# Layer ends with VectorE and ScalarE in a fixed order, and later step sums and norms in the SSD layer

## Chip, cores and metric

One core of a Trainium2 chip runs the whole program. The metric is the device time of one execution in microseconds; the median of three runs before the change is 2514.39 (2512.95 to 2517.65).

## What is computed

Two blocks of two layers each on 512 positions of 1024 channels, in float32. Block 1 has two equal layers:

```
h = rms_norm(x, pre_norm[layer]);  proj = h @ w_in[layer]      # conv half b,c,x,z and retention half q,k,v,z
y_conv = c_b * conv3(c_c * c_x) * silu(c_z)
y_ret  = rms(retention(rotary(q), rotary(k), v)) * silu(r_z)
out = concat(y_conv, y_ret) @ w_out[layer]
x = x + rms_norm(out, post_norm[layer])
```

Block 2 puts 16 meta tokens in front (528 positions) and computes an SSD mixer, an MLP, an attention and a second MLP. Its SSD mixer is the part that matters here:

```
z, xbc, dt = split(h @ w_in);  xbc = silu(conv4(xbc));  dt = softplus(dt + bias)
a_cs = cumsum(dt * a) per chunk of 128                          # the step sums
y = chunk-wise state recurrence over xs, B, C with decay exp(a_cs differences)   # 8 groups of 4 heads
g = (y + xs * d) * silu(z);  g = g * rsqrt(mean(g*g) over the group) * norm_g     # the norm of a group
return g @ w_out
```

## The kernel before

All weights stream from memory in tiles of 1 MB (`Stream`, two buffers each of the raw tile `wraw`, its leading part `whi`, cast by ScalarE at L74, and the rest `wlo`, a difference by VectorE at L75). A product is three matmuls: leading part by leading part and the two mixed terms. Activations are split in the same way (`xh`/`xl` in `prep`, L261 and L262; `mh`/`ml` in `split`, L418 and L419). A framework's scheduler puts the instructions of each engine in order; the order of program text counts only as far as it decides between ready instructions. PSUM has eight banks: `pb0` to `pb3` and the like for dense products, four `side` banks (`C0`, `C1`, `D0`, `D1`) for everything else.

**The end of a layer of block 1.** The last two tiles of the output product (`ob` 2 and 3) run in halves of 256 positions (`duo`): both tiles for the first half, then both for the second. VectorE adds each result to `oS` (L812). ScalarE squares it; the squares of output tiles 0 to 5 are summed by POOL (`sums`, L428), and three `ones` matmuls (L817, L820) sum over the channels. Then `residual` (from L774) does for one half: square root on ScalarE and reciprocal on VectorE (L438) give the factor `rp`; four pairs of channels are scaled (L782), added to the residual (L784) and split for the next layer (L261 on ScalarE, L262 on VectorE); squares of the new residual are added (`sqx`, L793), summed by two `ones` matmuls (L795) and become the next layer's factor `R` (`Rx` after layer 1). The next layer begins with its c and x tiles, again in halves (L390 is the matmul of all products in halves), drained by VectorE at L628 with the factor; the SSD layer begins likewise with `sx` and `sbc` (drains at L941).

**The SSD layer.** `steps` computes dt (VectorE's chain ends at L896), sums it by two matmuls (L899 with a triangle, L900 with ones) and sends the transposed sums through memory (`acsD`), from where each chunk's `ab` is broadcast. A group projects xs, B, C and z (L382, drains L853 and L958), then loops over five chunks: `cb` (L983), ScalarE's decay and VectorE's `M` (L989), `xd` (L992), matmuls of y (L1003), `xw` and state. Then the sum of squares goes through memory: `gd`, `rs`, twelve small VectorE steps (L405 to L409), `ge`, and the broadcast `rb` (POOL issues them at L1044 to L1049). At the end of the group, in program order, VectorE multiplies `gz` by the gain and `rb` (L1063) and splits it for the output product:

```
for n in range(2):
    V.scalar_tensor_tensor(gz[n], gz[n], gcol(V_SNG, 2 * g + n), rb, ALU.mult, ALU.mult)
    m = mix_tile(f"s{g}{n}")
    split(m, gz[n], slice(0, T2))
    mix.append(m)
```

Of the kernel before, what the change touches and what calls it, by code (L numbers as in the profile page):

```python
# [31 lines left out]
class Stream:  # L32
# [75 lines left out]
    def next(self, key):  # L108
        i = self.pos
        assert self.plan[i][0] == key, (self.plan[i][0], key)  # L110
        while len(self.done) <= min(i + 1, len(self.plan) - 1):
# [4 lines left out]
        return r


def build(ctx, tc, a):
# [331 lines left out]
    with ExitStack() as c1:  # L451
# [167 lines left out]

        for l in range(2):  # L620

            mixc = []
            for p in range(4):
                cR = [tmp(f"cR{l}{p}{n}") for n in range(2)]
                if p == 0:
                    for _, os_, u, pss in duo([(l, "c", 0), (l, "x", 0)], X, META, load_x if l == 0 else None):
# [44 lines left out]
                if p == 3:  # L671
# [102 lines left out]
            def residual(i, o0, o1):  # L774

                rp = tmp(f"rp{l}{o0}")[:, : o1 - o0]
                rsqrt_mean(rp, (C0, C1)[i][:, :256], D)
                xs = slice(META + o0, META + o1)
                sp_ = (D0, D1)[i][:, :256]
                for k in range(0, 8, 2):  # L780
                    o2 = oS[:, k : k + 2, o0:o1]
                    V.tensor_tensor(o2, o2, rp.unsqueeze(1).to_broadcast([P, 2, o1 - o0]), ALU.mult)  # L782
                    for j in (k, k + 1):
                        V.scalar_tensor_tensor(xres[:, j, xs], oS[:, j, o0:o1], gcol(V_POST, 8 * l + j),  # L784
                                               xres[:, j, xs], ALU.mult, ALU.add)
                        prep(Xn, j, xs, gcol(gbase, j))

                sq = tmp(f"sqx{l}0{o0}")
                for k in range(0, 8, 2):
                    t = tmp(f"sqx{l}{k}{o0}") if k else sq  # L790
                    nc.scalar.activation(t.rearrange("p (n c) -> p n c", n=2), xres[:, k : k + 2, xs], AF.Square)
                    if k:
                        V.tensor_tensor(sq, sq, t, ALU.add)  # L793
                for n in range(2):
                    nc.tensor.matmul(sp_, ones, sq[:, 256 * n : 256 * n + 256], start=(n == 0), stop=(n == 1))  # L795
                rsqrt_mean(R[:, o0:o1] if l == 0 else Rx[:, xs], sp_, D)
                if l == 0:
                    V.tensor_tensor(RR[:, o0:o1], R[:, o0:o1], R[:, o0:o1], ALU.mult)

# [8 lines left out]
            for i, os_, u, pss in duo([(l, "ob", 2), (l, "ob", 3)], mixop(mixr), 0):  # L808
                sp_ = (C0, C1)[i][:, :256]
                for n in range(2):  # L810
                    k = 4 + 2 * u + n
# [1 line left out]
                    if u == 0:
                        sq_acc(sqt, sums[:, os_], k, oS[:, k, os_], f"sqp{l}{k}{i}")
                        continue
                    if k == 6:
                        nc.tensor.matmul(sp_, ones, sums[:, os_], start=True, stop=False)  # L817
# [748 lines left out]
```

## Time and profile before

| | |
|---|---|
| median of three runs | 2514.39 us |
| the profiled execution, time | 2515.09 us |
| the profiled execution, span | 2513.2 us |
| TensorE busy | 2448.3 us (97%) |
| VectorE busy | 1619.0 us (64%) |
| ScalarE busy | 1077.6 us (43%) |
| POOL busy | 151.6 us (6%) |
| mean granted TensorE clock | 0.991 |

The span runs from the first to the last instruction of the profiled execution. Busy shares are means over the whole span; a wait in one place is seen in windows and in the timeline, not in them. The granted clock tells which share of its full rate of 2.4 GHz TensorE was given: 1.00, or 0.50 for 1.2 GHz.

### The profile page before, as it was taken

The page shows a single profiled execution, that of the slowest core. Times are in us where ns is not written, and L with a number is a line of the kernel's source. Part 1 is how long each engine was busy: PE and PEld are TensorE (multiplying, and loading weights), DVE is VectorE, ACT ScalarE, POOL GpSimd, SP SyncE. Part 2 cuts the span into 40 slices and gives each one's busy share as a digit, 9 for nine tenths or more (in the row PEclk, how much of TensorE's full clock was granted, in tenths as well). Part 3 has the DMA queues.
Part 4 walks back from the last instruction along what each step waited for, and adds up shares of the span by engine and source line. Part 5 has one row for each costly group of instructions (what it writes and reads, how often), then busy time and mean ns, then how long its engine had stood idle before and what let it go on. Part 6 is the DMA issues. An engine that isn't in the chain of part 4 may idle for free.

```text
span 2513.2 us, 40393 instructions
## 1 busy us (share of the span) xinstructions
PE 2448.3 (97%) x16671; PEld 2189.0 (87%) x16671; DVE 1619.0 (64%) x2968; ACT 1077.6 (43%) x2046; POOL 151.6 (6%) x177
## 2 busy tenths in 40 slices
PE   8999999989999999889999999999999999999999
PEld 7888888878888888778999998999998566999999
DVE  6743555474435554877857889677675666966764
ACT  4422333333223334455625546245354675644432
POOL 1000000100000001022302200000011000000000
PEclk9999999999999999998999999999999999999999
DMA  4333222223332222233333332233221221332322
GB/s 147 106 100 97 82 82 76 79 78 91 100 103 74 84 84 68 69 92 90 90 106 95 88 88 90 88 96 98 94 92 49 63 69 38 96 104 95 109 84 85
DMA packets 220488, 220.90 MB, mean 88 GB/s; under 512 B 8972, under 2 KB 212877, under 8 KB 220304
## 3 DMA queue, kind: packets, MB, share of 16 engines
q1 hardware_dynamic: 215648, 207.50, 26.9%
q0 software_dynamic: 4176, 10.69, 1.8%
q8 instruction: 131, 2.15, 0.3%
q14 instruction: 53, 0.43, 0.1%
q10 hardware_dynamic: 480, 0.13, 0.0%
HBM read 215.47 MB, written 2.83 MB: 87 GB/s over the span
## 4 chain that ended last, share of the span: by engine, by line
PE 83%; DVE 9%; ACT 3%; DMA 2%; issue 2%; POOL 1%; ACTq 0%; SPq 0%; DVEq 0%; POOLq 0%
PE pb L382 44%; PE main L397 7%; PE side L334 6%; PE pb L397 4%; PE main L382 3%; PE main L334 3%; PE pb L334 3%; PE pb L390 2%; PE side L1404 1%; PE side L1420 1%; DVE wlo L75 1%; PE side L1012 1%; PE side L1003 1%; ACT whi L74 1%; PE main L1409 1%
## 5 line engine op out<-in xcount | busy, mean ns | idle before, releaser
L74 ACT CAST whi<-wraw 128x1024 fp32r<-128x1024 f32 (+2 forms) x301 | 302.7, 1045 | 614.6 <-PE pb L382 421.8
L75 DVE TENSOR_TENSOR wlo<-wraw,whi 128x1024 fp32r<-128x1024 f32 (+2 forms) x301 | 364.2, 1232 | 121.5 <-ACT whi L74 119.2
L382 PE MATMUL pb<-xl_n,whi 128*128 128x264 f32 (+1 forms) x1136 | 317.9, 330 | 0.0
L382 PE MATMUL pb<-xh_n,whi 128*128 128x264 f32 (+1 forms) x1136 | 317.4, 329 | 0.3 <-DVE zu L958 0.2
L382 PE MATMUL pb<-xh_n,wlo 128*128 128x264 f32 (+1 forms) x1136 | 315.3, 329 | 0.0
L382 PEld LDWEIGHTS pb<-xh_n,whi 128*128 128x128 f32 x1136 | 192.5, 189 | 20.3 <-issue 1.6
L382 PEld LDWEIGHTS pb<-xl_n,whi 128*128 128x128 f32 x1136 | 191.6, 189 | 19.7 <-issue 1.7
L382 PEld LDWEIGHTS pb<-xh_n,wlo 128*128 128x128 f32 x1136 | 191.8, 190 | 17.6 <-issue 0.2
L382 PE MATMUL pb<-xl_l,whi 128*128 128x512 f32 x416 | 164.9, 396 | 0.0
L382 PE MATMUL pb<-xh_l,wlo 128*128 128x512 f32 x416 | 164.9, 396 | 0.0
L382 PE MATMUL pb<-xh_l,whi 128*128 128x512 f32 x416 | 164.5, 395 | 0.0
L397 PE MATMUL main<-whi,mh_w 128*128 128x256 f32 x512 | 143.8, 281 | 0.3
L397 PE MATMUL main<-whi,ml_w 128*128 128x256 f32 x512 | 143.3, 281 | 0.0
L397 PE MATMUL main<-wlo,mh_w 128*128 128x256 f32 x512 | 143.2, 281 | 0.0
L103 ACT CAST whi<-wraw 128x1024 fp32r<-128x1024 f32 x64 | 65.8, 1047 | 139.5 <-issue 54.5
L90 ACT CAST wsh<-wsr 128x512 fp32r<-128x512 f32 x96 | 58.8, 618 | 106.9 <-DVE wsr L96 64.0
L382 PE MATMUL pb<-ml_u,whi 128*128 128x264 f32 x512 | 104.2, 285 | 0.2
L382 PE MATMUL pb<-mh_u,whi 128*128 128x264 f32 x512 | 103.8, 284 | 0.0
L382 PE MATMUL pb<-mh_u,wlo 128*128 128x264 f32 x512 | 103.6, 284 | 0.0
L397 PEld LDWEIGHTS main<-whi,mh_w 128*128 128x128 f32 x512 | 96.6, 189 | 1.1 <-ACT mh_w L418 0.9
L397 PEld LDWEIGHTS main<-whi,ml_w 128*128 128x128 f32 x512 | 96.7, 189 | 0.0
L397 PEld LDWEIGHTS main<-wlo,mh_w 128*128 128x128 f32 x512 | 96.1, 188 | 0.0
(687 smaller groups left out, 6522.4 us busy)
## 6 DMA issues: line engine op xcount, KB each, us to landing
wraw<-w_in SPq DMA_DIRECT2D x63, 1024.0 KB, 5.8
wraw<-mlp_w_up SPq DMA_DIRECT2D x32, 1024.0 KB, 5.5
wraw<-mlp_w_down SPq DMA_DIRECT2D x32, 1024.0 KB, 4.8
wraw<-w_out SPq DMA_DIRECT2D x16, 1024.0 KB, 4.8
wraw<-ssd_w_in SPq DMA_DIRECT2D x16, 1024.0 KB
wraw<-ssd_w_in SPq DMA_DIRECT2D x16, 512.0 KB, 5.3
ab<-acsD POOLq DMA_DIRECT2D x32, 256.0 KB, 3.8
kR<-ke SPq DMA_DIRECT2D x32, 132.0 KB, 3.0
```

The costliest lines, as they stand in the source:

```text
L74: nc.scalar.copy(hv[s], rv[s])
L75: eng.tensor_tensor(lv[s], rv[s], hv[s].bitcast(F32), ALU.subtract)
L90: nc.scalar.copy(h, sr[:, n])
L103: nc.scalar.copy(hi[:, c], raw[:, c])
L334: nc.tensor.matmul(ps, w[wq][a][:, k], X(xq, b, k), start=(k == 0 and wq + xq == 0), stop=(k == 3 and wq == 1))
L382: nc.tensor.matmul(ps, w[wq][:, k, wsl], x(xq, k, cs), start=(k == 0 and wq + xq == 0), stop=(k == nk - 1 and wq == 1))
L390: nc.tensor.matmul(ps, w[wq][:, k, wsl], x(xq, k, cs), start=(k == 0 and wq + xq == 0), stop=(k == nk - 1 and wq == 1))
L397: nc.tensor.matmul(ps, x(xq, k, ts_), w[wq][:, k, csl], start=(k == 0 and wq + xq == 0), stop=(k == nk - 1 and xq == 1))
L1003: nc.tensor.matmul(o, xd[:W, h], M[:W, h, :W], start=True, stop=(c == 0))
L1012: nc.tensor.matmul(st[:, :256], Bt[:W], xw[:W].rearrange("p h e -> p (h e)"), start=True, stop=True)
L1404: nc.tensor.matmul(sp_, Qh[:, h, q0 : q0 + M], Kh[:, h, :L], start=True, stop=False)
L1409: nc.tensor.transpose(pst[:, c, :M], p[:M, P * c : P * c + P], ident[:M, :M])
```

## The change

Four things are rewritten.

1. `residual` becomes the class `End` with its steps (`chain`, `pair`, `squares`, `factor`) as separate methods. They are called between the matmuls of the last products and of the next layer's first ones (`mm3k` takes a callback `mid`). Squares of the last four output tiles are no longer added by POOL; `chain` sums five pieces by `ones` matmuls.
2. `Ordered` ties all VectorE instructions, and all ScalarE instructions, from the first half's chain to the drains of the next layer's first tiles (in layer 1: of the SSD layer's) to the order of the program text. `inorder` does the same for single instructions.
3. The first tiles of the next layer (`entry`) use four pairs of banks, `pb0`/`pb1`, `pb2`/`pb3`, and the `side` banks `C0`/`C1`, instead of whatever comes free.
4. The step sums become a generator that stops before the two sums and before the rest, so that the sums' matmuls come after both z products of group 0; and `finish`, the norm of a group, is called in the next group's chunk 1 (for group 3 before the first output pass).

```diff
+    def end(self):
...
+        for engine in (mybir.EngineType.DVE, mybir.EngineType.Activation):
+            mine = [i for i in traced[n + 1 :] if i.engine == engine]
+            for p, q in zip(mine, mine[1:]):
+                self.tc.add_manual_dep(q, p.name, mybir.DependencyInfo(mybir.DependencyClass.NoSync,
+                                                                       mybir.DependencyReason.DATA), reason="order")
...
+            def chain(self, sqs):
+                ps = (C0, C1)[self.i][:, :256]
+                for n, sq in enumerate(sqs):
+                    inorder(nc.tensor.matmul(ps, ones, sq, start=(n == 0), stop=(n == len(sqs) - 1)))
+                self.rp = tmp(f"rp{self.l}{self.i}")[:, :256]
+                rsqrt_mean(self.rp, ps, D)
+
+            def pair(self, k):
+                o2 = oS[:, k : k + 2, self.os]
+                V.tensor_tensor(o2, o2, self.rp.unsqueeze(1).to_broadcast([P, 2, 256]), ALU.mult)
+                for j in (k, k + 1):
+                    V.scalar_tensor_tensor(xres[:, j, self.xs], oS[:, j, self.os], gcol(V_POST, 8 * self.l + j),
+                                           xres[:, j, self.xs], ALU.mult, ALU.add)
+                for j in (k, k + 1):
+                    prep(self.X, j, self.xs, gcol(self.g, j))
...
+        def entry(keys, x, ends):
...
+            banks = [[BANK[b + n][:, : cols[0].stop - cols[0].start] for n in range(2)] for b in (0, 2, 4, 0)]
...
+            mm(0, 0, (6, lambda: ends[1].chain(ends[1].sqs)))
+            for k in range(0, 8, 2):
+                ends[1].pair(k)
+                if k == 0:
+                    ends[0].squares()
+            if l:
+                yield
+            mm(1, 0)
+            ends[0].factor()
+            for u in range(2):
+                yield 0, slice(*PARTS[0]), u, banks[u]
+            ends[1].squares()
+            mm(0, 1)
+            ws.emit(len(ws.done))
+            ends[1].factor()
+            mm(1, 1)
+            for u in range(2):
+                yield 1, slice(*PARTS[1]), u, banks[2 + u]
+            order.end()
...
+            def first_end():
+                ends[0].chain(sqs)
+                order.begin()
+                ends[0].pair(0)
+
+            sqs1 = [sums[:, ends[1].os]] + last(1, 0, (2, first_end))
+            ends[0].pair(2)
+            ws.emit(len(ws.done))
+            ends[0].pair(4)
+            ends[1].sqs = sqs1 + last(1, 1)
+            ends[0].pair(6)
+            ws.emit(len(ws.done))
...
+            yield
             cs_ps = D0
-            nc.tensor.matmul(cs_ps[:, :160], tri, e_, start=True, stop=True)
+            inorder(nc.tensor.matmul(cs_ps[:, :160], tri, e_, start=True, stop=True))
...
+                if c == 1 and late:
+                    late.pop()()
...
-            for n in range(2):
-                V.scalar_tensor_tensor(gz[n], gz[n], gcol(V_SNG, 2 * g + n), rb, ALU.mult, ALU.mult)
-                m = mix_tile(f"s{g}{n}")
-                split(m, gz[n], slice(0, T2))
-                mix.append(m)
+            def finish(g=g, gz=gz, rb=rb):
+                for n in range(2):
+                    inorder(V.scalar_tensor_tensor(gz[n], gz[n], gcol(V_SNG, 2 * g + n), rb, ALU.mult, ALU.mult))
...
+            if g == 7:
+                finish()
+            else:
+                late.append(finish)
```

How the instructions move, in three places.

VectorE at the end of layer 0, from the first half's last pair on. In the kernel before, `sqx` is the first half's sum of squares, `R` the next layer's factor, `rp` the factor of the second half, L812 the drain of the last output tiles and `wlo` a weight tile:

```order
L784 SCALAR_TENSOR_TENSOR xres<-oS,vec,xres 128x256 x2
L793 TENSOR_TENSOR sqx_3662<-sqx_3662,sqx_3664 128x512
L262 SCALAR_TENSOR_TENSOR xl_n_3373<-xres,vec,xh_n_3371 128x256 x2
L793 TENSOR_TENSOR sqx_3662<-sqx_3662,sqx_3667 128x512
L812 TENSOR_TENSOR oS<-pb_77,oS 128x256
L793 TENSOR_TENSOR sqx_3662<-sqx_3662,sqx_3670 128x512
L812 TENSOR_TENSOR oS<-pb_77,oS 128x256
L812 TENSOR_TENSOR oS<-pb_78,oS 128x256 x2
L75 TENSOR_TENSOR wlo_3841<-wraw_3842,whi_3840 128x1024 x2
L438 RECIPROCAL R<-R 128x256
L438 RECIPROCAL rp_3791<-rp_3791 128x256
L798 TENSOR_TENSOR CR<-R 128x256
```

and now (L660 is the scaling before L782, L662 L784, L282 L262, L674 L793):

```order
L660 TENSOR_TENSOR oS<-oS,rp_3633 128x2x256
L662 SCALAR_TENSOR_TENSOR xres<-oS,vec,xres 128x256 x2
L282 SCALAR_TENSOR_TENSOR xl_n_3373<-xres,vec,xh_n_3371 128x256 x2
L75 TENSOR_TENSOR wlo_3767<-wraw_3768,whi_3766 128x1024 x2
L460 RECIPROCAL rp_3817<-rp_3817 128x256
L660 TENSOR_TENSOR oS<-oS,rp_3817 128x2x256
L662 SCALAR_TENSOR_TENSOR xres<-oS,vec,xres 128x256 x2
L282 SCALAR_TENSOR_TENSOR xl_n_3372<-xres,vec,xh_n_3370 128x256 x2
L674 TENSOR_TENSOR sqx_3839<-sqx_3839,sqx_3841 128x512
L674 TENSOR_TENSOR sqx_3839<-sqx_3839,sqx_3844 128x512
L674 TENSOR_TENSOR sqx_3839<-sqx_3839,sqx_3847 128x512
```

The second half's `rp` now comes right behind the first half's pairs and a weight tile; the first half's three `sqx` additions stand behind the second half's first pair, and its reciprocal of `R` behind all pairs of the second half.

TensorE at the step sums, before (`wlo_7580` and `whi_7579` are the z tile, L899 and L900 the sums, L910 their transposes):

```order
L382 MATMUL pb_77<-xh_n_6854,whi_7579 128x264 x2
L382 MATMUL pb_77<-xl_n_6856,whi_7579 128x264 x2
L382 MATMUL pb_77<-xh_n_6854,wlo_7580 128x264 x2
L899 MATMUL side_72<-sf_7645,tri 128x160
L900 MATMUL side_72<-sf_7645,ones 128x160
L910 MATMUL side_73<-ident,acs 32x128 x2
L910 MATMUL side_72<-ident,acs 32x16
```

and now (L996 and L997 are the sums, L1007 the transposes; `whi_7676` is the tile behind z):

```order
L402 MATMUL pb_78<-xh_n_6850,wlo_7677 128x264 x2
L402 MATMUL pb_78<-xh_n_6850,whi_7676 128x264
L996 MATMUL side_72<-sf_7637,tri 128x160
L997 MATMUL side_72<-sf_7637,ones 128x160
L402 MATMUL pb_78<-xh_n_6850,whi_7676 128x264
L402 MATMUL pb_78<-xl_n_6852,whi_7676 128x264 x2
L402 MATMUL pb_78<-xh_n_6850,wlo_7677 128x264 x2
L1007 MATMUL side_73<-ident,acs 32x128
L402 MATMUL pb_78<-xh_n_6850,whi_7676 128x264 x2
```

The sums stood right behind the z products; now 37 matmuls of the next product stand ahead of them, and the transposes between further ones.

VectorE from group 0 to group 1, before (L1063 is the norm of group 0, `M_0`, `xw_0` and what else has `_0` are group 1's chunk 0):

```order
L996 TENSOR_TENSOR eb_2_8474<-eb_2_8474,Cs_8270 128x512
L1063 SCALAR_TENSOR_TENSOR gz_7817<-gz_7817,vec,rb_7990 128x528
L1063 SCALAR_TENSOR_TENSOR gz_7818<-gz_7818,vec,rb_7990 128x528
L419 TENSOR_TENSOR ml_s_8024<-gz_7817,mh_s_8023 128x528
L958 TENSOR_TENSOR zu_8387<-pb_77,Rx 128x528
L419 TENSOR_TENSOR ml_s_8029<-gz_7818,mh_s_8028 128x528
L983 TENSOR_TENSOR cb_0_8399<-side_72,tri 16x16
L992 TENSOR_TENSOR xd_0_8408<-side_72,dt 16x256
L960 SCALAR_TENSOR_TENSOR sz_8338<-sz_8338,zu_8387 128x528
L989 TENSOR_TENSOR M_0_8401<-M_0_8401,cb_0_8399 16x4x16
L1008 TENSOR_TENSOR xw_0_8414<-side_72,wd 16x256
```

and now (L1088 is `M`, L1167 the norm; `_1` is group 1's chunk 1):

```order
L1109 TENSOR_TENSOR xw_0_8394<-side_72,wd 16x256
L75 TENSOR_TENSOR wlo_8589<-wraw_8590,whi_8588 128x1024
L1057 SCALAR_TENSOR_TENSOR sz_8320<-sz_8320,zu_8369 128x528
L75 TENSOR_TENSOR wlo_8589<-wraw_8590,whi_8588 128x1024
L1082 TENSOR_TENSOR cb_1_8407<-side_72,tri 128x128
L1091 TENSOR_TENSOR xd_1_8416<-side_72,dt 128x256
L1088 TENSOR_TENSOR M_1_8409<-M_1_8409,cb_1_8407 128x512
L1167 SCALAR_TENSOR_TENSOR gz_7909<-gz_7909,vec,rb_7982 128x528
L1109 TENSOR_TENSOR xw_1_8439<-side_72,wd 128x256
L441 TENSOR_TENSOR ml_s_8420<-gz_7909,mh_s_8419 128x528
L1167 SCALAR_TENSOR_TENSOR gz_7910<-gz_7910,vec,rb_7982 128x528
L1120 TENSOR_TENSOR pv_1_8444<-side_73,pv_1_8444 128x256
```

The norm of group 0 stood ahead of all of group 1's chunks and of the drain of its second z product; now it stands behind `M` of chunk 1.

## Rows read from the trace of the kernel before

**Rows 1.** The page, part 1: busy us (share of the span) and instructions of the engine.

```profile
PE 2448.3 (97%) x16671; PEld 2189.0 (87%) x16671; DVE 1619.0 (64%) x2968; ACT 1077.6 (43%) x2046; POOL 151.6 (6%) x177
```

**Rows 2.** Busy time by window; PEclk is TensorE's granted clock; columns: window, length, engines, PEclk, DMA.

```profile
508.30:513.30 5.00, 0.15 (x2) 0.14 (x2) 5.00 (x12) 4.38 (x8) 0.20 (x1) 1.00 0.65 195
513.30:519.40 6.10, 4.13 (x11) 2.77 (x11) 4.67 (x6) 1.53 (x4) 3.38 (x2) 0.51 0.26 63
520.90:531.60 10.70, 10.67 (x92) 10.43 (x90) 10.70 (x23) 5.40 (x12) 0.00 (x0) 1.00 0.04 15
531.60:545.50 13.90, 12.23 (x101) 12.15 (x102) 8.08 (x13) 2.80 (x4) 0.00 (x0) 1.00 0.05 15
1009.80:1014.70 4.90, 0.05 (x2) 0.04 (x1) 4.90 (x12) 4.37 (x8) 0.11 (x1) 0.70 0.09 13
1066.80:1069.90 3.10, 1.17 (x6) 0.66 (x5) 3.00 (x7) 1.85 (x2) 0.00 (x0) 0.98 0.49 173
1069.90:1076.70 6.80, 5.20 (x23) 4.03 (x24) 5.35 (x15) 1.82 (x4) 0.51 (x1) 0.51 0.55 165
1124.50:1130.70 6.20, 0.11 (x3) 0.03 (x2) 4.62 (x10) 3.69 (x5) 0.00 (x0) 0.77 0.06 15
1130.70:1138.00 7.30, 7.30 (x34) 6.37 (x35) 4.07 (x7) 2.60 (x8) 1.38 (x2) 0.50 0.48 123
1179.70:1182.70 3.00, 1.56 (x16) 1.24 (x15) 3.00 (x8) 2.72 (x7) 0.00 (x0) 0.95 0.00 0
1182.70:1189.00 6.30, 6.30 (x26) 5.61 (x26) 3.25 (x6) 1.62 (x5) 1.36 (x2) 0.50 0.55 164
```

**Rows 3.** Waits, 495 to 550 and 1060 to 1195: total us, times, longest.

```profile
PE side L795 <- DVE sqx L793: 4.9, 1, 4.9
...
DVE gz L1063 <- DMA rb<-ge: 7.5, 2, 4.4
PE side L1003 <- DVE M L989: 7.5, 2, 6.1
```

**Rows 4.** VectorE's timeline, ends of the stretch at the end of layer 0.

```profile
498.09 1.75 DVE L438 RECIPROCAL rp<-rp 128x256 f32<-128x256 f32 x1 [1.91 <-ACT rp L437]
...
531.71 0.48 DVE L262 SCALAR_TENSOR_TENSOR xl_n<-xres,vec,xh_n 128x256 fp32r<-128x256 f32 x1
```

**Rows 5.** Instruction groups, 495 to 546: count | busy us, mean ns | idle before.

```profile
L75 DVE TENSOR_TENSOR wlo<-wraw,whi 128x1024 fp32r<-128x1024 f32 x6 | 7.1, 1216 | 0.2 <-ACT whi L74 0.2
L784 DVE SCALAR_TENSOR_TENSOR xres<-oS,vec,xres 128x256 f32<-128x256 f32 x16 | 7.0, 478 | 0.0
L262 DVE SCALAR_TENSOR_TENSOR xl_n<-xres,vec,xh_n 128x256 fp32r<-128x256 f32 x16 | 7.0, 478 | 0.0
L782 DVE TENSOR_TENSOR oS<-oS,rp 128x512 f32<-128x512 f32 x8 | 5.2, 684 | 0.0
L793 DVE TENSOR_TENSOR sqx<-sqx,sqx 128x512 f32<-128x512 f32 x6 | 4.1, 682 | 0.0
L795 PE MATMUL side<-sqx,ones 128*128 128x256 f32 x8 | 2.9, 502 | 4.9 <-DVE sqx L793 4.9
L812 DVE TENSOR_TENSOR oS<-pb,oS 128x256 f32<-128x256 f32 x6 | 2.2, 412 | 4.9 <-PE pb L390 4.9
```

**Rows 6.** POOL's timeline, group 0 to 1.

```profile
1117.15 0.50 POOL L1048 DMA_DIRECT2D ge<-rs  x1 [10.36 <-DVE rs L409]
1122.36 0.55 POOL L1049 DMA_DIRECT2D rb<-ge  x1 [4.71 <-DMA ge<-rs]
```

**Rows 7.** VectorE's timeline, group 0 to 1.

```profile
1126.06 1.45 DVE L1063 SCALAR_TENSOR_TENSOR gz<-gz,vec,rb 128x528 f32<-128x528 f32 x2 [4.43 <-DMA rb<-ge]
```

**Rows 8.** VectorE's groups over the span, norm products and splits.

```profile
L1063 DVE SCALAR_TENSOR_TENSOR gz<-gz,vec,rb 128x528 f32<-128x528 f32 x16 | 11.6, 764 | 11.0 <-DMA rb<-ge 10.7
L419 DVE TENSOR_TENSOR ml_s<-gz,mh_s 128x528 fp32r<-128x528 f32 x16 | 10.7, 701 | 0.0
```

**Rows 9.** TensorE's waits, 1192 to 1500.

```profile
PE side L1003 <- DVE M L989: 1.3, 1, 1.3
```

More of the change, by code (lines that the diff above doesn't have):

```diff
@@ L122, in build @@
     out = a["out"]
+    inorder = tc.keep_in_program_order
     cp = ctx.enter_context(tc.tile_pool(name="cp", bufs=1))
@@ new lines, in build, with mm @@
+        order = Ordered(tc)
+        def entry(keys, x, ends):
+            us = [ws.next(key, 0) for key in keys]
+            l = ends[0].l
+            cols = HS if l else [slice(META + o0, META + o1) for o0, o1 in PARTS]
+            banks = [[BANK[b + n][:, : cols[0].stop - cols[0].start] for n in range(2)] for b in (0, 2, 4, 0)]
+            def mm(u, i, mid=None):
+                mm3k([(banks[2 * i + u][n], us[u], slice(P * n, P * n + P), cols[i]) for n in range(2)], x, 8, mid)
+            mm(0, 0, (6, lambda: ends[1].chain(ends[1].sqs)))
+            for k in range(0, 8, 2):
+                ends[1].pair(k)
[15 more added lines that the diff above has]
+            order.end()
@@ L772, in build @@
                     prep(Xn, k, slice(0, META), gcol(gbase, k))
[L774 to L793, printed above, removed]
-                for n in range(2):
[L795 to L798, printed above, removed]
+            ends = [End(i, l, Xn, gbase) for i in range(2)]
             for q in range(2):
@@ L807, in build, with last @@
                     sq_acc(sqt, sums, k, oS[:, k], f"sqo{l}{k}")
-            for i, os_, u, pss in duo([(l, "ob", 2), (l, "ob", 3)], mixop(mixr), 0):
-                sp_ = (C0, C1)[i][:, :256]
+            wo = [ws.next((l, "ob", 2)), ws.next((l, "ob", 3), 0)]
+            def last(i, u, mid=None):
+                os_ = ends[i].os
+                pss = [acc()[:, :256] for n in range(2)]
+                mm3k([(pss[n], wo[u], slice(P * n, P * n + P), os_) for n in range(2)], mixop(mixr), 8, mid)
+                res = []
                 for n in range(2):
@@ L812, in build @@
                     V.tensor_tensor(oS[:, k, os_], pss[n], oS[:, k, os_], ALU.add)
[L813 to L817, printed above, removed]
-                    sq = sqt(f"sqp{l}{k}{i}")[:, :256]
-                    nc.scalar.activation(sq, oS[:, k, os_], AF.Square)
-                    nc.tensor.matmul(sp_, ones, sq, start=False, stop=(k == 7))
-                if u == 1:
-                    residual(i, os_.start, os_.stop)
+                    if n == 0:
+                        sq = sqt(f"sqp{l}{u}{i}")
+                    res.append(sq[:, 256 * n : 256 * n + 256])
+                    nc.scalar.activation(res[n], oS[:, k, os_], AF.Square)
+                return res
+            sqs = [sums[:, ends[0].os]] + last(0, 0)
+            sqs += last(0, 1)
+            def first_end():
[9 more added lines that the diff above has]
+            ws.emit(len(ws.done))
             X = Xn
+        first = entry([("sx", 0), ("sbc", 0)], X, ends)
+        next(first)
     def dense2(w, n, x, nk):
@@ L912, in steps @@
             nc.gpsimd.dma_start(acsD, aT)
+            yield
         mix = []
+        late = []
         def out_pass(i, mix, js, X=None):
@@ L961, in build @@
                 sz.append(t)
+                if g + n == 0:
+                    next(st_)
             if g == 4:
+                late.pop()()
                 out_pass(0, mix, range(4))
                 mix = []
-            gz = [tmp(f"gz{g}{n}", "gz", 3) for n in range(2)]
             prev = None
@@ L1020, in build @@
                     prev = nx
+                if c == 2:
+                    gz = [tmp(f"gz{g}{n}", "gz", 3) for n in range(2)]
                 if c in (2, 4):
```

66 lines of the change are left out of this document (49 added, 17 removed).

## Prediction

> **What bounds the kernel now.** First the page: TensorE is busy 97% of the span [rows 1], so time can only come from the places where it stands still or runs at half clock. I looked for them by cutting the span into windows and reading busy time and granted clock together [rows 2]. In the five places that the change touches the reader is to see the same picture: an idle stretch, and after it a stretch in which TensorE is busy at a granted clock of 0.50, its 1.2 GHz level instead of 2.4. What is lost there is the idle time plus half of the busy time at 0.50:
>
> - end of layer 0: 4.85 us idle from 508.3, then 6.1 us with 4.13 busy at 0.51 (4.0 lost), and 1.67 after 531.6; about 10.5.
> - end of layer 1: the same picture 501.5 us later, 4.85 idle again; I take 10.5 for it too.
> - the step sums of the SSD layer (1066.8 to 1076.7): 1.9 + 4.2 = 6.1.
> - SSD group 0 to 1 (1124.5 to 1138.0): 6.1 + 3.65 = 9.7.
> - SSD group 1 to 2 (1179.7 to 1189.0): 1.4 + 3.15 = 4.6.
>
> Together 41.4 us, about the most that the change could return. Next, who is late: the waits [rows 3]. At a layer's end TensorE waits for VectorE's sum `sqx`; at group 0 to 1 it waits up to 6.1 us for VectorE's tile `M`, and VectorE itself had been standing 4.4 us at `gz` (L1063) for a DMA, the broadcast norm factor `rb`. So VectorE holds up everything behind one late DMA. Last I read what VectorE does from the first half's reciprocal to the last pair of the second half [rows 4]: 498.09 to 532.19, 34.1 us nearly without a pause. That stretch, not TensorE, sets the end of a layer.
>
> **Layer ends.** Per half the change sums five pieces by `ones` matmuls, three before: two more of 0.502 [rows 5], 1.0 us, and the POOL additions go. The factor's reciprocal, which followed at 498.09, starts at about 499.6 (1.0 for the matmuls, 0.5 because the last square now precedes the chain). In the fixed order VectorE then has, up to the last pair: two reciprocals of 1.75, eight pairs, four drains of 0.412, four weight differences of 1.216 and three additions of 0.682. A pair is one product of 0.684, two of 0.478 and two of 0.478 [rows 5], 2.6 us, and in the new order each `xl_n` follows directly on the ScalarE cast that it needs, so nothing of it overlaps. Before, four pairs ran mixed with one another. Sum 3.5 + 20.8 + 1.6 + 4.9 + 2.0 = 32.8 us, so the last pair ends at 499.6 + 32.8 = 532.4, where it was 532.19. VectorE gains nothing.
>
> TensorE does: c and x of the first half run in the idle stretch from 508.6 on (pairs 0 to 6 are there in time but for some small waits), up to about 523. Then c of the second half follows VectorE, a pair of matmul steps (12 matmuls of 0.116, [rows 2], 520.9 to 531.6: 92 in 10.67) in 1.4 us for each 2.6 of VectorE, four waits of about 1.3 us. c ends at 532.4 + 1.4 = 533.8; x of the second half takes the banks of the first c, whose drains now stand behind the factor's reciprocal, so it starts about 1.6 us later and ends, with its two factor matmuls, at about 542.9, where it was 545.5: 2.6 us gained. Two things take it back. In the new order two matmuls of the z product stand ahead of those of b and wait for the next weight tile's cast, 1.3 us. And the four waits leave TensorE busy about half the time, as it was from 1179.7 to 1182.7 (1.56 of 3.0), after which the clock fell for 6.3 us [rows 2]; while VectorE leads, the low clock costs little (12 matmuls then take 2.8 against 2.6), the rest I put at 1.3. **Layer 0: 0**, bounds -2.6 (neither happens) and +4 (the clock is down for x too, 48 matmuls of 0.116 once more, less what a start half-way recovers).
>
> Layer 1's end has the same steps, but its second half leads into the SSD layer, where there are more banks and dt follows without the z detour: 4.4 us by my step-through less 1.3 for the clock. **Layer 1: -3**, bounds -4.4 and +1.
>
> **Step sums.** They were issued right after the second z product, where VectorE was not ready; now 37 of 48 matmuls of the next product stand between. The idle and half-clock time of 6.1 can go. What is late next is the drain of z: the banks are taken again sooner, and I count waits of 1.8 and 1.2 there. **-3**, bounds -6.1 and 0.
>
> **Norms of the SSD groups.** `gz` with its split moves behind `M_1` of the next group's chunk loop. Its cover there is the dense work of that next group. At group 0 to 1 the chain behind `rb` keeps its time: POOL issues `ge` at 1117.15 and `rb` at 1122.36, and VectorE starts `gz` at 1126.06 [rows 6, 7]. TensorE comes earlier by what was gained above, so VectorE can again stand at `gz`, 0.4 to 3.3 us by my steps, now with TensorE's lead of a projection ahead of it, so 0 to 1.6 us idle for TensorE; if that drops the clock, 3.2 more. **-5**, bounds -9.7 and -2. Where a DMA is still late, the same queue stands as before: behind `gz` are `xw` and `pv` of chunk 1 and all of chunk 2. Group 1 to 2: by the new order 19 VectorE instructions stand between the end of the `rs` steps and `gz`, where there are 11 at group 0 to 1, and the wait should go. **-4**, bounds -4.6 and 0. Later groups waited almost nowhere (1.3 us on `M` in 300 us, [rows 9]): 0. One load of the MLP's weights on SP's queue changes place; it stands a tile ahead of its use: 0. The eight POOL additions that go were waited for only in the chains above.
>
> **Sum.** 0 - 3 - 3 - 5 - 4 = -15. The profiled execution took 2515.09 (span 2513.2), 0.7 above the median of 2514.39: 2515.1 - 15 = **2500**. The lower ends add up to -27, the upper ones to +3.
>
> **Rivals.**
>
> *All covers hold* (0.20). Every term at its lower end: 2515.1 - 27 = 2488. For it: the idle stretches are single waits with other work at hand. Against it: VectorE's 34 us at a layer's end are not shortened.
>
> *The clock stays down through both layer ends* (0.13). One idle time of 1.44 in group 1 to 2 was enough to bring the level down for 6.3 us; four waits in a row could hold it down from the first half's c to the second half's x. 192 matmuls then take 192 x 0.232 = 44.6 us from 508.6 on, against the 37.2 that they took with their stop: +7.5 at each end, +15 - 3 - 5 - 4 = +3, or 2518; if only half of it happens, 2510. Against it: 1.67 us of idle after 531.6 left the clock at 1.00. The Trainium skill ("TensorE: Matmul & The Clock Gate", section "A second HAM failure mode: psum-queue depth-cycling") tells of small idle times between groups of matmuls, often enough to make the clock swing between its levels. By that rule this rival, not the forecast, would be the case.
>
> *The late norms hold the chunk loop* (0.09, slower). `finish` puts two products of 0.764 and two differences of 0.701 [rows 8], 2.93 us of VectorE, into the chunk loops of six groups, between `M_1` and `M_2`. Before, they lay under the next group's projections. If TensorE's lead over `M` in the loop is under 2.9 us, each of the six gets longer by up to that: 6 x 2.93 = 17.6, and at group 0 to 1, where VectorE stands at `rb` as well, nothing is gained: 2515.1 - 0 - 3 - 3 - 4 + 17.6 = 2523. For it: VectorE works through its queue in order, as its stand at `rb` with `M` behind it shows [rows 3]. Against it: from group 2 on TensorE hardly waits for `M` [rows 9].
>
> *The order doesn't change*, since a scheduler decides it: the instruction orders above show that it does. No chance.
>
> **Chances.** Forecast 0.58, all covers 0.20, clock 0.13, norms 0.09. A measurement of this kernel can tell 0.2%, about 5 us, from no change. The first two are faster, the third lies around no change, the fourth is slower: 0.78, 0.13, 0.09. The range 2484 to 2511 takes in the forecast with its bounds and the covers; outside lie the norms (0.09), most of the clock's case (0.08) and a little below.
>
> **What will show it.** Layer 0's end: VectorE's last pair near 532, TensorE's four waits of about 1.3 us before it, x ending near 543 and a granted clock under 1 around 525 to 540. Step sums: the `tri` matmul without a wait, no stretch at 0.50 behind it. Group 0 to 1: no 6 us wait on `M`; VectorE's wait at `gz` up to 3.3 us. I am wrong if the windows at the layer ends lose more than 12 us each, or if groups 2 to 7 show new waits for `M`.

## The result and the profile after

The changed kernel takes 2501.88 us (median of four runs, 2500.41 to 2502.59) against 2514.55 before: a ratio of 0.9947, 95% interval 0.993 to 0.9965. The forecast was 2500.

The page of the changed kernel, part 1 (busy us, share, instructions), has four us less of busy TensorE than [rows 1], although it has eight `ones` matmuls more; the rest of the 13.6 us by which its span is shorter is idle time.

```profile
PE 2444.5 (98%) x16687; PEld 2184.2 (87%) x16687; DVE 1623.8 (65%) x2968; ACT 1074.4 (43%) x2046; POOL 147.5 (6%) x169
```

The same windows as [rows 2], now of the changed kernel, shifted to where its stages lie (columns as there; PEclk is the third number from the end):

```profile
508.30:513.30 5.00, 4.87 (x39) 4.47 (x38) 4.78 (x10) 1.49 (x4) 0.00 (x0) 1.00 0.43 102
524.00:534.40 10.40, 7.29 (x43) 5.41 (x42) 9.57 (x18) 4.62 (x11) 0.00 (x0) 1.00 0.00 0
534.40:545.20 10.80, 7.71 (x56) 6.96 (x56) 10.38 (x18) 5.27 (x8) 0.00 (x0) 1.00 0.21 54
1024.00:1034.00 10.00, 7.27 (x45) 5.71 (x44) 8.67 (x18) 4.22 (x10) 0.00 (x0) 1.00 0.02 6
1063.30:1074.00 10.70, 9.07 (x67) 8.20 (x66) 10.06 (x25) 4.23 (x7) 0.00 (x0) 1.00 0.63 196
1115.00:1130.00 15.00, 11.59 (x63) 10.07 (x61) 12.63 (x32) 7.15 (x14) 2.43 (x4) 0.66 0.29 90
1166.00:1176.00 10.00, 10.00 (x84) 9.15 (x83) 9.77 (x18) 6.08 (x12) 2.13 (x3) 1.00 0.41 129
```

The reader is to see three things. The stop at 508.3 is gone (4.87 busy of 5.00, was 0.15), but TensorE now has holes later, from 524 to 545. The clock stays at 1.00 at both layer ends and at the step sums; of the five places it falls at one only, group 0 to 1 (0.66 from 1115 to 1130). And group 1 to 2 has no hole left. TensorE's waits at the end of layer 0, from its timeline (start, length, instruction, and in brackets the idle time before it and who ended it):

```profile
525.62 0.70 PE L681 MATMUL side<-sqx,ones 128*128 128x256 f32 x2 [1.28 <-DVE sqx L674]
...
527.28 0.50 PE L412 MATMUL side<-xh_n,whi 128*128 128x256 f32 x2 [0.53 <-ACT xh_n L281]
...
529.86 0.50 PE L412 MATMUL side<-xh_n,whi 128*128 128x256 f32 x2 [0.63 <-ACT xh_n L281]
...
532.45 0.50 PE L412 MATMUL side<-xh_n,whi 128*128 128x256 f32 x2 [0.61 <-ACT xh_n L281]
...
536.35 0.39 PE L412 MATMUL pb<-xh_n,whi 128*128 128x256 f32 x1 [1.94 <-DVE cR L729]
...
544.22 0.51 PE L402 MATMUL pb<-xh_n,whi 128*128 128x512 f32 x1 [1.06 <-ACT whi L74]
```

c of the second half waits three times for ScalarE's casts, 0.53, 0.63 and 0.61; the 1.28 ahead of these is at the `ones` matmul of the first half's factor, which stands between c's matmuls and waits for `sqx`. x then waits 1.94 for the drains, and the next tile 1.06. That tile starts at 544.22, where it was 545.5 [rows 2]. At group 0 to 1 the wait of 6.1 on `M` [rows 3] has become one of 2.54 at the matmul of B and C and one of 0.87 on `M`, because VectorE, which had stood 4.43 us at `gz` [rows 7], now stands 4.71 at the first of the small `rs` steps for the transfer ahead of it (before, 2.43 there); `gz` itself no longer waits. VectorE's timeline, and TensorE's:

```profile
1114.36 0.16 DVE L1149 TENSOR_SCALAR rs<-rs 48x11 f32<-48x11 f32 x1 [4.71 <-DMA rs<-gd]
...
1117.40 0.71 DVE L958 SCALAR_TENSOR_TENSOR Cs<-uCs,Cs 128x528 f32<-128x528 f32 x1
...
1127.60 0.76 DVE L1167 SCALAR_TENSOR_TENSOR gz<-gz,vec,rb 128x528 f32<-128x528 f32 x1
```

```profile
1118.17 0.21 PE L1076 MATMUL side<-Cs,Bs 128*16 128x16 f32 x2 [2.54 <-DVE Cs L958]
...
1121.39 0.61 PE L1104 MATMUL side<-M,xd 16*64 16x16 f32 x8 [0.87 <-DVE M L1088]
```

### The profile page after: what moved, and what is told of

It reads as the page before. It is cut to its first block, busy times and chain, and to the rows that moved or that the text cites. A ratio compares the mean times of both kernels' runs of the same rounds, so it can differ in the third digit from the quotient of the medians.

```text
span 2499.6 us, 40373 instructions
## 1 busy us (share of the span) xinstructions
PE 2444.5 (98%) x16687; PEld 2184.2 (87%) x16687; DVE 1623.8 (65%) x2968; ACT 1074.4 (43%) x2046; POOL 147.5 (6%) x169
## 4 chain that ended last, share of the span: by engine, by line
PE 85%; DVE 8%; ACT 3%; issue 1%; DMA 1%; POOL 1%; ACTq 0%; DVEq 0%; SPq 0%; POOLq 0%
PE pb L402 47%; PE main L419 7%; PE side L354 6%; PE pb L419 4%; PE main L402 3%; PE main L354 3%; PE pb L354 3%; PE pb L412 2%; PE side L1513 1%; DVE wlo L75 1%; PE side L1529 1%; ACT whi L74 1%; PE side L1104 1%; PE main L1518 1%; PE side L1113 1%
```

## The experiments

Twelve kernels were run. The table gives for each the median, the ratio to the kernel before measured beside it, and four times from its trace: the first matmul of dt (the end of layer 1's second half), and the starts of VectorE's product `M` in chunk 0 of group 0 and in the last chunks of groups 1 and 2. The last three tell at which place time was won or lost; all four come from one profiled execution of each kernel, so differences of some tenths of a us say little. The kernel before, measured beside each set, had medians of 2514.91 (e1 to e4), 2517.39 (e5 to e8) and 2513.56 (e9 to e12), so kernels of different sets are compared by the ratio. Most kernels ran four times, within 2 to 7 us of one another; e2_steps and e4_ends ran ten times and spread over 13 and 14 us.

| kernel | median us | ratio [95%] | dt | M, group 0 | M, group 1 end | M, group 2 end |
|---|---|---|---|---|---|---|
| before | 2514.55 | | 1048.59 | 1082.42 | 1148.96 | 1199.94 |
| changed | 2501.88 | 0.9947 [0.993, 0.9965] | 1045.12 | 1082.40 | 1142.03 | 1188.45 |
| e1_norms | 2501.16 | 0.995 [0.9933, 0.9968] | 1048.50 | 1082.32 | 1139.89 | 1186.36 |
| e2_steps | 2509.40 | 0.9974 [0.996, 0.9987] | 1048.44 | 1084.14 | 1145.82 | 1197.31 |
| e3_both | 2499.46 | 0.9942 [0.9927, 0.9957] | 1048.75 | 1084.17 | 1140.46 | 1186.88 |
| e4_ends | 2521.41 | 1.0019 [1.0007, 1.0032] | 1045.05 | 1083.15 | 1149.66 | 1195.58 |
| e5_free | 2492.22 | 0.99 [0.9881, 0.9919] | 1034.38 | 1072.16 | 1129.73 | 1176.23 |
| e6_rs | 2501.98 | 0.9939 [0.9923, 0.9954] | 1046.60 | 1084.02 | 1141.27 | 1187.22 |
| e7_chain | 2505.93 | 0.9954 [0.9939, 0.9969] | 1046.74 | 1087.50 | 1145.40 | 1191.83 |
| e8_all | 2506.24 | 0.9956 [0.9941, 0.9971] | 1045.22 | 1085.79 | 1143.55 | 1189.99 |
| e9_nosteps | 2492.66 | 0.9909 [0.9895, 0.9924] | 1034.44 | 1071.95 | 1129.51 | 1175.92 |
| e10_banks | 2503.91 | 0.9954 [0.9939, 0.9969] | 1047.59 | 1084.36 | 1140.21 | 1186.86 |
| e11_chain3 | 2485.65 | 0.9882 [0.9866, 0.9899] | 1035.71 | 1072.50 | 1124.43 | 1170.87 |
| e12_act | 2501.31 | 0.9944 [0.9929, 0.9959] | 1041.04 | 1078.21 | 1139.43 | 1185.94 |

### One part of the change alone

**e1_norms**, the kernel before with the third part:

```diff
+                if c == 1 and late:
+                    late.pop()()
...
+            def finish(g=g, gz=gz, rb=rb):
+                for n in range(2):
+                    inorder(V.scalar_tensor_tensor(gz[n], gz[n], gcol(V_SNG, 2 * g + n), rb, ALU.mult, ALU.mult))
```

> Kernel before plus the late norms alone (finish in the next group's chunk 1). My theory: the wait of 6.1 us on M at group 0 to 1 and the one of 1.4 at group 1 to 2 shrink with the half-clock stretches behind them; layer ends and step sums stay as before (TensorE idle 4.9 us from 508.3, 0.50 clock after 1069.9). Total 2515 - 8 = about 2506, VectorE's lead of the chunk loops 6 to 8 us from group 1 on and 3 more from group 2. Rival (late norms hold the chunk loops): new waits on M of up to 2.9 us in each of six groups, 2515 or more. Rival (the layer ends bring the gain, not the norms): under 3 us, 2512 or more.

It fell by as much as the whole change. `M` stands at 1082.32 in group 0, as before, is 9.1 us earlier at the end of group 1 and 13.6 at that of group 2. The late norms hold no loop: TensorE waits for no `M` from 1085 to 1135. VectorE now waits for the transfer ahead of the `rs` steps, 19.2 us in six groups, where nothing hangs on it. VectorE's waits on these transfers, 1055 to 1500, in e1_norms:

```profile
DVE rs L1053 <- DMA rs<-gd: 19.2, 6, 3.4
```

**e2_steps**, the kernel before with the late step sums, and **e3_both**, with both:

```diff
+            yield
             cs_ps = D0
-            nc.tensor.matmul(cs_ps[:, :160], tri, e_, start=True, stop=True)
+            inorder(nc.tensor.matmul(cs_ps[:, :160], tri, e_, start=True, stop=True))
...
+                if g + n == 0:
+                    next(st_)
```

> Kernel before plus the late step sums alone. My theory: the 6.1 us of idle and half-clock time at the step sums go, but group 0's chunk loop starts on M at the same time as before and the norm factor rb of group 0 lands at the same time, so what TensorE gains is lost again at the 6 us wait of group 0 to 1: 2513 to 2515, and the M instructions of group 1 less than 1 us earlier than before. Rival (each part pays for itself): 2509 to 2511, M of group 1 from 3 to 6 us earlier.

> Kernel before plus late step sums and late norms; layer ends as before. My theory: the lead gained at the step sums now passes group 0 to 1, so the two together give more than their sum: about 11 of the 12.7 us, 2503 to 2505, with the layer ends good for 1 to 2 us only. Rival (the layer ends carry several us): 2506 or more, as late norms alone. Rival (parts add up): the sum of the two single runs.

Alone the late sums gave more than my theory expected, 2509.4, as the rival had it. Group 0's `M` starts 1.7 us later than before, as the sums do; but TensorE no longer stands at the sums, and at group 0 to 1 it waits 2.81 for `Cs` and 1.16 for `M` in place of 6.1 [rows 3]. A part of this goes again at group 1 to 2, where it waits 4.05 and had waited 1.4. TensorE's waits on `M` in e2_steps, 1055 to 1190, then its timeline at the three waits from group 0 to 2:

```profile
PE side L1009 <- DVE M L995: 7.2, 3, 4.0
```

```profile
1120.10 0.22 PE L983 MATMUL side<-Cs,Bs 128*16 128x16 f32 x2 [2.81 <-DVE Cs L863]
...
1123.32 0.61 PE L1009 MATMUL side<-M,xd 16*64 16x16 f32 x8 [1.16 <-DVE M L995]
...
1179.22 0.41 PE L1009 MATMUL side<-M,xd 16*64 16x16 f32 x8 [4.05 <-DVE M L995]
```

With the late norms in place that is worth little: e3_both and e1_norms have overlapping intervals, and `M` at the end of group 2 is 0.5 later. In e3_both TensorE does not stand at the sums, but waits 3.1 us for `M` and 1.4 for `Cs`, where e1_norms has no such wait: the time won at the sums is waited for at the next places.

**e4_ends**, the changed kernel with step sums and norms put back, so with the layer ends alone:

```diff
-            yield
             cs_ps = D0
...
-                if c == 1 and late:
-                    late.pop()()
```

> The changed kernel with step sums and norms as before: only the layer ends in their fixed order, with the five-piece chain and the extra banks. My theory: x of the second half ends 2 to 4 us earlier at both ends; of this layer 0 keeps 0.5 to 1, and the second end's lead is swallowed by the wait for rb at group 0 to 1: 2513 to 2514. Rival (the layer ends pay in full): 2509 to 2511.

It is slightly slower than before, which neither my theory nor the rival had. dt starts 3.5 us earlier, as in the changed kernel, and `M` of group 0 0.7 later: the lead is gone within the step sums, where TensorE now waits 5.83 us for VectorE's last step (1.22 before). Later groups lose more, since VectorE's wait for `rb` comes back for the norms of groups 5 and 6 (13.2 us in seven waits, 10.7 in five before, [rows 8]). TensorE's timeline in e4_ends at the sums, then VectorE's waits, 1055 to 1500:

```profile
1069.15 0.90 PE L995 MATMUL side<-sf,tri 128*128 128x160 f32 x2 [5.83 <-DVE sf L992]
```

```profile
DVE gz L1159 <- DMA rb<-ge: 13.2, 7, 4.1
```

### What the layer ends lose

**e5_free** drops the fixed order and leaves all else:

```diff
     def end(self):
+        return
         traced = self.nc.cur_bb.bb.instructions
```

> The changed kernel without the fixed order of VectorE and ScalarE (Ordered.end adds nothing): methods, banks, chain, step sums and norms as changed. My theory: the layer ends are bound by VectorE's 33 us in either order, so x of the second half ends within 1.5 us of 543.2 at layer 0 and the total stays within 3 us of the changed kernel (2499 to 2505). Rival (the order by hand is what makes the end work): x of the second half ends 3 us later or more at both ends, total 2505 or more.

My theory fell, and not on the rival's side: without the order the kernel is 10 us faster than the changed one. dt starts at 1034.38, 10.7 us ahead of the changed kernel. At the end of layer 0, x of the second half ends at 537.8, where it was 543.2. In the changed kernel VectorE waits at every pair for the ScalarE cast, and twice for a weight tile's; in e5_free the scheduler has mixed the pairs, and there is no such wait. From 499 to the last pair these waits, with one for ScalarE's `sqx`, come to 2.9 us. The rest lies in the order of the steps: the changed kernel's last three pairs follow one another every 2.58 us, while the five steps of a pair, mixed with those of another, take about 2.2 in e5_free (an estimate from its starts: 0.60 for a product and 0.40 for each of the other four). VectorE's timeline of the changed kernel, two of its eight pairs and a tile, then TensorE's of e5_free, with all of its waits between 508 and 536:

```profile
502.76 0.89 DVE L282 SCALAR_TENSOR_TENSOR xl_n<-xres,vec,xh_n 128x256 fp32r<-128x256 f32 x2 [0.18 <-ACT xh_n L281]
...
506.00 0.89 DVE L282 SCALAR_TENSOR_TENSOR xl_n<-xres,vec,xh_n 128x256 fp32r<-128x256 f32 x2 [0.18 <-ACT xh_n L281]
507.35 2.36 DVE L75 TENSOR_TENSOR wlo<-wraw,whi 128x1024 fp32r<-128x1024 f32 x2 [0.46 <-ACT whi L74]
...
523.28 2.28 DVE L674 TENSOR_TENSOR sqx<-sqx,sqx 128x512 f32<-128x512 f32 x3 [0.56 <-ACT sqx L672]
```

```profile
528.98 0.39 PE L413 MATMUL side<-xl_n,whi 128*128 128x256 f32 x1 [1.31 <-DVE xl_n L283]
...
530.98 0.38 PE L413 MATMUL pb<-xh_n,whi 128*128 128x256 f32 x1 [0.56 <-DVE cR L730]
```

**e12_act** fixes ScalarE's order only:

```diff
-        for engine in (mybir.EngineType.DVE, mybir.EngineType.Activation):
+        for engine in (mybir.EngineType.Activation,):
```

> The changed kernel with the fixed order on ScalarE only; VectorE's order is left to the scheduler. My theory: it is VectorE's fixed order that costs (each xl_n stands right behind the ScalarE cast that it needs, so VectorE waits or leaves gaps in all eight pairs); without it the total is within 2 us of e5_free, 2490 to 2494. Rival (ScalarE's order costs, since casts of weight tiles stand ahead of the squares): 2499 to 2503 as the changed kernel.

The rival was right on the total. At the layer ends both orders cost: dt starts at 1041.04, so ScalarE's order alone takes 6.7 of the 10.7 us and VectorE's 4.1 more (VectorE's alone was not run). ScalarE squares four `sqx` tiles in a row, 2.18 us from 520.65, behind the second half's first two casts; in e5_free it squares three of them from 515.32. So the square root of the first half's factor comes at 528.41 and not at 524.04, VectorE reaches the drains late, and x waits 2.76 for them. Of the 4.1 us that e12_act has ahead of the changed kernel at dt, 2.6 are left at the end of group 1 and nothing that the medians show at the end of the program. ScalarE's timeline of e12_act and of e5_free at this square root, then TensorE's of e12_act, where x starts:

```profile
528.41 0.45 ACT L459 ACTIVATE R<-side,eps 128x256 f32<-128x256 f32 x1
```

```profile
524.04 0.45 ACT L460 ACTIVATE R<-side,eps 128x256 f32<-128x256 f32 x1
```

```profile
532.88 0.58 PE L412 MATMUL pb<-xh_n,whi 128*128 128x256 f32 x1 [2.76 <-DVE cR L729]
```

**e10_banks** is e5_free without the third pair of banks:

```diff
-            banks = [... for b in (0, 2, 4, 0)]
+            banks = [... for b in (0, 2, 0, 2)]
```

> As e5_free, but the second half's c goes back to the banks of the first half's c instead of the side banks. My theory: c of the second half then waits for the drains that stand behind the first half's factor (R), which VectorE reaches late, so TensorE stops 2 to 6 us at each layer end: 2496 to 2503. Rival (the extra banks are not needed, since the second half waits for VectorE's pairs anyway): 2490 to 2494.

The banks pay, and more than expected: c of the second half waits 7.87 us for the drains of the first at layer 0, dt starts 13.2 us later than in e5_free, and the ratio is 0.9954 instead of 0.99. TensorE's timeline of e10_banks:

```profile
530.68 0.55 PE L413 MATMUL pb<-xh_n,whi 128*128 128x256 f32 x1 [7.87 <-DVE cR L730]
```

**e9_nosteps** is e5_free with the step sums as before (the edit of e2_steps taken back):

> The changed kernel without the fixed order (as e5_free) and with the step sums as before the change; late norms and rewritten layer ends stay. My theory now: layer ends without the fixed order pay about 5 us each, late norms about 13, and the late step sums 1 to 3; so 2493 to 2496, with TensorE idle some 5 us at the step sums and a half-clock stretch behind it. Rival (late sums only delay group 0's loop, by 1.7 us as in e2_steps): 2489 to 2491.

No difference: 2492.66 and 2492.22, with overlapping intervals of the ratio, and `M` within 0.3 us at all three places. The late step sums, with the other parts in place, return nothing that can be measured, although TensorE's granted clock from 1056 to 1066 is 0.53 in e9_nosteps and 1.00 in e5_free. Where the time goes again is seen in TensorE's waits: e9_nosteps stands 5.83 us at the sums and has no wait on `M` or `Cs` up to the end of group 1; e5_free does not stand at the sums, but waits 2.03 for `M` of group 0, and at group 0 to 1 2.56 for `Cs` and 1.37 for `M`. The window of e9_nosteps and of e5_free, then TensorE's timeline of e9_nosteps at the sums and of e5_free:

```profile
1056.00:1066.00 10.00, 6.40 (x28) 4.63 (x29) 6.88 (x21) 1.81 (x4) 0.51 (x1) 0.53 0.51 167
```

```profile
1056.00:1066.00 10.00, 9.67 (x71) 8.23 (x70) 8.92 (x24) 3.01 (x7) 0.51 (x1) 1.00 0.53 172
```

```profile
1058.28 0.90 PE L996 MATMUL side<-sf,tri 128*128 128x160 f32 x2 [5.83 <-DVE sf L993]
```

```profile
1072.42 0.41 PE L1105 MATMUL side<-M,xd 16*64 16x16 f32 x8 [2.03 <-DVE M L1089]
...
1107.92 0.21 PE L1077 MATMUL side<-Cs,Bs 128*16 128x16 f32 x2 [2.56 <-DVE Cs L959]
...
1111.14 0.41 PE L1105 MATMUL side<-M,xd 16*64 16x16 f32 x8 [1.37 <-DVE M L1089]
```

### The step chain and the norm's transfers

**e7_chain** ties weight differences, z drain and the Cs convolution behind VectorE's last step of the sums:

```diff
+            for i in traced[n:]:
+                if i.engine == dve and any(t in repr(i) for t in ("wlo", "zu0", "Cs0")):
+                    tc.add_manual_dep(i, last.name, mybir.DependencyInfo(mybir.DependencyClass.NoSync,
+                                                                         mybir.DependencyReason.DATA), reason="behind")
```

> The changed kernel with VectorE's chain of the step sums in one piece (weight differences, z drain and Cs convolution of that stretch tied behind its last step). My theory: this chain is where the lead of layer 1's end is lost (its first step is 2.9 us earlier than before the change, its last 1.3 later, because three weight differences of 1.2 us and others stand between its steps). In one piece its last step comes near 1065 instead of 1069, M of group 0 2 to 4 us earlier, and the total falls by 1 to 4 us to 2498 to 2501. Rival (group 0's loop waits for something else, the ab transfers): M of group 0 stays at 1082 to 1083 and the total too.

The chain did what it should: its last step stands at 1064.60 instead of 1068.98. But the z drain behind it is late now, TensorE waits 4.11 us for it, POOL sends the transposed sums at 1076.31 instead of 1074.38 and can fetch them 5.6 us after that instead of 2.8. `M` of group 0 is 5.1 later, of which 1.6 had been there at dt. The chain was not the only thing that holds group 0; what took its place cost more. VectorE's timeline of e7_chain, the seven dependent steps and the last one, then TensorE's wait:

```profile
1061.08 2.48 DVE L986 SCALAR_TENSOR_TENSOR sf<-sf,sf 128x160 f32<-128x160 f32 x7
...
1064.60 0.33 DVE L992 SCALAR_TENSOR_TENSOR sf<-dt,ea 128x160 f32<-128x160 f32 x1
```

```profile
1069.90 0.39 PE L402 MATMUL pb<-xh_n,whi 128*128 128x264 f32 x1 [4.11 <-DVE zu L1068]
```

**e6_rs** issues the small norm steps after the next group's Cs convolution, **e8_all** does both:

```diff
+                def factor(rs=rs, rm=rm, rt_=rt_, d2=d2, rb=rb):
+                    inorder(V.tensor_scalar(rm, rm, 1.0 / 1024.0, EPS, ALU.mult, ALU.add))
...
+            if early:
+                early.pop()()
             w = ws.next(("sz", g))
```

> The changed kernel with the small norm steps (rs) and the two transfers behind them issued after the next group's Cs convolution instead of at the group's end. My theory: VectorE's stand of 4.7 us on rs<-gd at 1114 goes, with it TensorE's wait of 2.5 us for Cs and the half-clock stretch 1115 to 1125; the lead on M in group 1 and later grows by 2 to 5 us, total 2497 to 2500. Rival (the wait only moves on to rb): VectorE stands at gz for rb by several us, total 2501 or more.

> Both of the last two: small norm steps after Cs, and the step chain in one piece. My theory: the lead of the layer end passes both places, so 2494 to 2498, 2 or more below either alone. Rival: no better than the better of the two.

VectorE's stand of 4.7 became one of 1.6 and TensorE's wait for Cs went, but the total did not move: `M` of group 0 is 1.6 later in this kernel, since dt already starts 1.5 later (why was not looked into), and of the time won in group 1 about 1 us is left. e8_all has no gain either. The place is real, this edit doesn't collect it.

**e11_chain3** is e5_free with three pieces in the chain and POOL's additions for tiles 4 and 5:

```diff
+                    if u == 0:
+                        sq_acc(sqt, sums[:, os_], k, oS[:, k, os_], f"sqp{l}{k}{i}")
+                        continue
```

> As e5_free, but the squares of the output tiles 4 and 5 are added by POOL again, and three pieces go through the ones matmuls instead of five. My theory: TensorE has 2.0 us less to do per layer and waits for POOL about as long, so 2490 to 2494, no difference; at the second half's chain POOL's addition is hidden behind c. Rival (the POOL additions were what the chain waited for): 2495 or more.

This is the fastest kernel of all, 1.2% below the kernel before. Its interval of the ratio still overlaps that of e5_free, which belongs to another set; beside e9_nosteps of its own set, which takes as long as e5_free, it is 7.0 us faster. The reason is another than the edit's: dt and `M` of group 0 are 1.3 and 0.3 us later than in e5_free, and the 5.3 us are won between groups 0 and 1. There VectorE waits 0.40 us for the transfer ahead of the `rs` steps and 4.69 in e5_free. Both wait for the same 2.1 KB. In e5_free POOL issues them at 1099.15, 0.28 us behind the load of a weight tile, as in the changed kernel (0.31 behind); in e11_chain3 POOL issues them at 1098.38, 0.81 ahead of that load. First VectorE's timeline in e5_free and in e11_chain3, then SyncE's at the load in both, then for each the window from the transfer's issue to the step (the last two columns are the share of DMA busy and GB/s):

```profile
1104.11 0.16 DVE L1150 TENSOR_SCALAR rs<-rs 48x11 f32<-48x11 f32 x1 [4.69 <-DMA rs<-gd]
```

```profile
1100.15 0.16 DVE L1153 TENSOR_SCALAR rs<-rs 48x11 f32<-48x11 f32 x1 [0.40 <-DMA rs<-gd]
```

```profile
1098.87 0.37 SPq L61 DMA_DIRECT2D wraw<-ssd_w_in  x1
```

```profile
1099.19 0.37 SPq L61 DMA_DIRECT2D wraw<-ssd_w_in  x1
```

```profile
1099.10:1104.10 5.00, 5.00 (x43) 5.00 (x42) 0.32 (x1) 0.00 (x0) 0.55 (x1) 1.00 0.67 210
```

```profile
1098.40:1100.20 1.80, 1.80 (x17) 1.80 (x16) 1.40 (x3) 0.00 (x0) 0.53 (x1) 1.00 0.02 2
```

From issue to step the transfer takes 5.0 us at a DMA share of 0.67 and 1.8 at 0.02. Why the loads leave this gap here was not tried. That the gap pays and not the number of pieces, e7_chain bears out: it has five pieces, the same transfer took 1.8 us from issue to landing in it, and TensorE has no wait on `Cs` or `M` between groups 0 and 1 either. What three pieces do by themselves is not shown beyond the 1.3 us that dt loses.

## Why the prediction was right, and where its steps were not

The total came out within 2 us, and that is partly luck. Two terms of 3 us each, layer 1 and the step sums, returned nothing up to `M` of group 0. The norms returned 11.5 in place of 9, and 2.1 us of the 13.6 by which the span is shorter came after group 2, where I had put 0.

- **Layer 0: 0, bounds -2.6 and +4.** Right. The start of the next tile moved by 1.3 us, of which 0.3 had been there at 477 us, ahead of the change's first instruction. Pairs end at 533.3 (forecast 532.4), x at 543.2 (542.9). Of the four waits of 1.3 at c's pairs there are three, of about 0.6; the one that is 1.3 long stands at the `ones` matmul of the first half's factor, which I had not counted as a wait.
- **"VectorE gains nothing."** True of the order that was written, and the reason was in the text: "in the new order each `xl_n` follows directly on the ScalarE cast that it needs, so nothing of it overlaps". What I did not see is that this is a price of the fixed order and not of the work. e5_free shows it, with 5.4 us at the end of layer 0.
- **The clock.** I put 1.3 us at each end for a falling clock, and the rival had it down throughout. The granted clock stayed at 1.00 from 524 to 534 with 7.29 of 10.4 us busy and four waits; before the change it had fallen after 1.56 busy of 3.0 [rows 2]. So what the Trainium skill ("TensorE: Matmul & The Clock Gate", section "A second HAM failure mode: psum-queue depth-cycling") tells of another kernel, that small idle times between groups make the clock swing, did not come true at the layer ends here.
- **Layer 1: -3.** dt was 3.5 us earlier, as forecast, but the term failed one step later: `M` of group 0 starts at 1082.40, 0.02 us earlier than before. From dt to `M` it is 33.8 us before and 37.3 in the changed kernel, and 36.8 to 38.1 in e4_ends, e5_free and e9_nosteps to e12_act. So it is not that a lead runs into something fixed (of the 14.2 us that e5_free leads at dt, 10.3 arrive at `M`): with the rewritten ends this stretch itself takes 3 to 4 us longer. I had let the lead run on into the SSD layer without asking what VectorE still has to do there. What takes longer is its chain of the step sums: from dt to the chain's last step it is 19.1 us before and 23.9 in the changed kernel. Before, seven dependent steps ran in one piece of 2.49 us; in the changed kernel weight differences stand between them. That this alone costs the lead is not shown, since e7_chain, which puts the chain in one piece, was slower. VectorE's timeline of the kernel before, with the last step, then of the changed one:

```profile
1064.20 2.49 DVE L890 SCALAR_TENSOR_TENSOR sf<-sf,sf 128x160 f32<-128x160 f32 x7
...
1067.71 0.33 DVE L896 SCALAR_TENSOR_TENSOR sf<-dt,ea 128x160 f32<-128x160 f32 x1
```

```profile
1061.47 0.31 DVE L986 SCALAR_TENSOR_TENSOR sf<-sf,sf 128x160 f32<-128x160 f32 x1
...
1062.57 1.21 DVE L75 TENSOR_TENSOR wlo<-wraw,whi 128x1024 fp32r<-128x1024 f32 x1
1063.70 0.30 DVE L986 SCALAR_TENSOR_TENSOR sf<-sf,sf 128x160 f32<-128x160 f32 x1
...
1064.79 1.21 DVE L75 TENSOR_TENSOR wlo<-wraw,whi 128x1024 fp32r<-128x1024 f32 x1
...
1068.98 0.33 DVE L992 SCALAR_TENSOR_TENSOR sf<-dt,ea 128x160 f32<-128x160 f32 x1
```

- **Step sums: -3.** The idle and half-clock time went, as the window from 1063.3 to 1074 shows, but what TensorE gains there it waits for later (1.32 us on `M` of group 0, and at group 0 to 1): e9_nosteps has the stop at the sums back and takes as long as e5_free. The term should have been 0 beside the late norms.
- **Norms, group 0 to 1: -5, group 1 to 2: -4.** Mis-sized. Alone (e1_norms) they are worth 9.1 and 4.5 us of `M`, nearly all that stood in the windows of before (9.7 and 4.6); in the changed kernel 6.9 and 4.6. The late DMA that I looked for at `gz` (0.4 to 3.3 us) struck one transfer earlier, at the `rs` steps, which stood ahead of the Cs convolution: 4.71 us of VectorE, 2.54 of TensorE, and a half-clock stretch behind it.
- **The slower rival**, late norms in the chunk loop, did not come true in any kernel that has them.

Measured on `M`, of the 12.3 us that are won at group 4 none had been won by group 0, 6.9 were at the end of group 1, and 11.5 at that of group 2. So the norms are the change, as e1_norms shows, which has them alone and takes as long as the changed kernel; the layer ends with their order give nothing, and alone they lose 0.2%. The fastest versions keep the late norms, the rewritten ends and the banks, and drop the order by hand.

## What to carry to other kernels

An order pinned by hand should be compared with the same program unpinned: here the program text and the banks were worth 10 us more without the pins. A lead that TensorE wins at one place has to be followed along the late engine to the next: here 3.5 us at dt were none at `M`. And a wait that holds up an engine's other work should be moved behind everything that doesn't need it, with all of its chain: VectorE stood 4.71 us at the small `rs` steps, ahead of the Cs convolution, as it had stood 4.43 at `gz`.

## What was not expected of the hardware

A transfer of 2.1 KB took 1.8 us from issue to its reader with the DMA engines idle, and 5.0 while a weight tile of 1 MB was moving (0.67 of the engines busy, 210 GB/s). And the clock held at 2.4 GHz through ten us in which TensorE was busy for 7.29 of 10.4.
